# One core, a hybrid decoder trunk: values and probabilities turned through DRAM in another key order, and the first norm's gains carried in x's own rows

## The chip, the cores and the metric

The kernel runs on one core of a Trainium2 chip. A core has TensorE (matrix products, called PE in the profile, with its weight loads as PEld), VectorE (DVE), ScalarE (ACT), GpSimd (POOL) and SyncE (SP), which share an on-chip memory of 128 partitions and 16 DMA engines. DMAs are issued from the queues of SP, ACT and POOL. The metric is the time of one execution on the device, in microseconds; less is better.

## What is computed

A trunk of two layers on 272 tokens (16 learned meta tokens and 256 of the input), width 2048, 16 heads of 128. Layer 0 is forgetting attention and a squared-ReLU MLP; layer 1 is stick-breaking attention with its own shared keys and values, and another MLP. The final norm is given out for the 256 tokens.

```python
def rms_norm(x, g):
    y = x * lax.rsqrt(jnp.mean(x * x, axis=-1, keepdims=True) + RMS_EPS)
    return y * g
...
h = concatenate([meta_tokens, x])                       # 272 x 2048
for layer in range(2):
    a = rms_norm(h, norm_attn[layer])
    if layer == 0:                                      # forgetting attention
        q, k, v, f_logit = split(a @ fox_w_in[0])
        cum_logf = cumsum(log_sigmoid(f_logit + fox_b_f[0]))
        p = softmax(q k / sqrt(128) + cum_logf[query] - cum_logf[key], keys up to the query)
        h = h + (p v) @ fox_w_o[0]
    else:                                               # stick-breaking attention
        k, v = split(rms_norm(h, kv_norm) @ w_kv)
        z = (a @ sb_w_q[0]) k / sqrt(128)
        p = exp(log_sigmoid(z) + sum of log_sigmoid(-z) over later keys before the query)
        h = h + (p v) @ sb_w_o[0]
    h = h + square(relu(rms_norm(h, norm_mlp[layer]) @ w_up[layer])) @ w_down[layer]
return rms_norm(h, final_norm)[16:]
```

In both attentions p v is a sum over keys. It comes out the same in any order of the keys, as long as p and v have the same one.

## The kernel before, in words

**Activations** stand with features on the partitions: `hT` is the residual stream, 16 chunks of 128 features by 272 tokens in float32. A norm is split in two: the gain is multiplied onto a chunk when it is split for the products (`split_chunk`), and the factor per token is multiplied onto the results.

**Products.** Every float32 operand is split into a rounded part (hi) and the rest (lo), and three products hi·hi, hi·lo, lo·hi replace one. Weights come as blocks of 128 x 512 by DMA on SP's queue (`raw`), ScalarE makes `whi` (L210), VectorE `wlo` (L211). A `gemm_group` is 512 output features: four quarters `kb` of the input features, 48 products each, 192 in all, with all tokens as the moving columns: 272 in layer 0 and for layer 1's keys and values, 256 (without the meta tokens, `t0 = M`) elsewhere in layer 1. A few products are issued six columns wider, on zeros beside the row (`wide`). Groups are numbered by `u` in program order: 1 to 12 are layer 0's q, k, v, 13 to 16 its output projection, 17 to 48 its MLP, 49 to 52 layer 1's queries, 53 to 60 its keys and values, 61 to 64 its output projection, 65 on its MLP. The last group is computed with tokens on the partitions (`token_group`).

**Order.** The framework's planner orders the instructions of each engine by simulated times. The code ties it down: products of a group (but for the first) keep their order, and other instructions are put behind the product with a given number of the group (`behind(ins, issued[140])`).

**The start.** Nine idle products on a constant (each two passes in the trace) run on TensorE before the data is there (L61). In the first group `load_x` (L314) issues x's chunks on SP's queue in turn with the weights, and the gains of all six norms (`g_sb`, L318) right after x's first chunk; the first block of weights goes on ACT's queue (L197). `load_gates` (L336) loads the forget gates' bias and weights on ACT's queue in the second quarter and multiplies the gate weights by the first norm's gains; their products come after the first group.

**Heads.** Heads are worked in four groups of four, each as two pairs. Values come out of the products with features on the partitions, while p v needs keys there. VectorE turns 32 x 32 squares (`squares`, `turn_probabilities`), and a trip through DRAM moves the squares: `scratch` writes the values of a pair (`turned` to `v_dram`) with four DMAs, one for every 32 partitions, in pieces of 512 bytes; `values_read` reads them back as 128 rows of 2 KB; `values_back` splits them. Probabilities go the same way, `turn_probabilities` (four DMAs a pair) and `probabilities_back`, with pieces of 768 bytes and rows of 3 KB. In layer 0 both use POOL's queue, in layer 1 the probabilities use SP's. The weighted sums of a group (`po`) are computed during a later group. The last four heads of a layer have no later attention group: `last_heads` puts their reads, splits and products between the products of the first group of the output projection, at given numbers (`reads`, `uses`, `places`). That projection needs the results (`x_o`) of the first pair from product 144 on and of the second pair from 168 on. In layer 1 the second pair of the last heads is written from ACT's queue. `to_token_major` uses `scratch` too, for the last 512 features of the residual stream.

Of the kernel before, what the change touches and what calls it, by code (L numbers as in the profile page):

```python
# [15 lines left out]
P = 128  # L16
# [17 lines left out]
def yoco_kernel(ctx: ExitStack, tc: tile.TileContext, hT_in, gains, b_f, w_f, w_qkv0, w_o0, w_up, w_dn,  # L34
# [16 lines left out]

    hT = const.tile([P, NC, T], F32, name="hT")
    g_sb = const.tile([P, 6, NC], F32, name="g_sb")
# [5 lines left out]
    idle = patt.tile([P, 512], F32, tag="patt", name="idle")  # L59
    for _ in range(9):  # L60
        nc.tensor.matmul(idle[:, :P], mean_w, mean_w, start=True, stop=True)  # L61
# [60 lines left out]
    def split_chunk(sp, gi, c):  # L122

        g = g_sb[:, gi, c:c + 1]
        nc.scalar.activation(sp.hi[:, c], hT[:, c, sp.t0:], AF.Copy, scale=g)
        nc.vector.scalar_tensor_tensor(out=sp.lo[:, c], in0=hT[:, c, sp.t0:], scalar=g,
                                       in1=sp.hi[:, c].bitcast(F32), op0=ALU.mult, op1=ALU.subtract)
# [87 lines left out]
    def gemm_group(wblk, sp, t0, evac, before={}, after={}, load_x=None, between={}):  # L215
# [7 lines left out]
        for kb in range(4):  # L223
# [16 lines left out]
            for kcs, ms in runs:  # L240
# [6 lines left out]

                wide = [(0, 0, 0), (1, 0, 1), (2, 1, 1)] if t0 and u % 4 == 1 else []
                if u == 61:
# [64 lines left out]
    def load_x(chunks):  # L314
        c0, n = chunks[0], len(chunks)
        nc.sync.dma_start(hT[:, c0:c0 + n, :], hT_in[:, c0:c0 + n, :])
        if c0 == 0:
            nc.sync.dma_start(g_sb, gains)  # L318
        for c in chunks:
            split_chunk(xa, G_A0, c)  # L320
# [15 lines left out]
    def load_gates(wf_sb, wf, both):  # L336
        nc.scalar.dma_start(bf_sb, b_f)
        nc.scalar.dma_start(wf_sb, w_f)
        nc.vector.tensor_tensor(out=wf[:, :, :NC], in0=wf_sb, in1=g_sb[:, G_A0, :].unsqueeze(2).to_broadcast([P, NC, NC]), op=ALU.mult)

# [51 lines left out]
    def scratch(t, products, queues=(nc.gpsimd, nc.gpsimd)):  # L392
        for pr in range(2):
            y = t[:, pr].rearrange("p (c x) -> p c x", c=4)
            for a in range(4):
                ins = queues[pr].dma_start(v_dram[pr].rearrange("c j a x -> a j c x")[a], y[32 * a:32 * a + 32])
                behind(ins, products[pr])

    def values_read(t, pr, read, queue=nc.gpsimd):
        ins = queue.dma_start(t[:, pr], v_dram[pr].rearrange("c j a x -> (c j) (a x)"))  # L400
        behind(ins, read)
        return ins.ins
# [66 lines left out]
    def turn_probabilities(s, raw, pr, queue):  # L469

        y = raw[:, :768].rearrange("p (c h b i) -> p c h b i", c=4, h=2, b=3)
        for i in range(2):
            for b, o in enumerate((0, 144, 144 + P)):
                nc.vector.transpose(y[:, :, i, b, :], s[:, 2 * pr + i, o:o + P].rearrange("p (c k) -> p c k", c=4))
        y = y.rearrange("p c h b i -> p c (h b i)")
        for a in range(4):
            queue.dma_start(p_dram[pr].rearrange("c j a x -> a j c x")[a], y[32 * a:32 * a + 32])

    def probabilities_back(pps, places, queue):
        for pr, at in enumerate(places):  # L480
            raw, p0 = pps[pr]
            behind(queue.dma_start(raw[:, :768], p_dram[pr].rearrange("c j a x -> (c j) (a x)")), issued[at])

# [258 lines left out]
    for g in range(4):  # L742
# [43 lines left out]
        turned = squares(vT, "pp", f"1_{g}")  # L786
        if g < 3:
            scratch(turned, issued[-2:])
        else:
            scratch(turned, (issued[-20], issued[-1]), (nc.gpsimd, nc.scalar))  # L790

# [47 lines left out]

    box["last"] = last_heads(turned, (36, 60), (84, 116), (120, 146), "1_3", nc.gpsimd, pair1, corner1)  # L840

# [11 lines left out]
    def to_token_major():  # L853
        t = squares(hT[:, 12:, M:], "pp", "h")
        scratch(t, issued[-2:])
        return t
# [131 lines left out]
```

## Time and profile before

| | |
|---|---|
| median of 3 runs | 2265.85 us (2265.61 to 2266.42) |
| the profiled execution | 2264.61 us, its span 2262.9 us |
| TensorE's products, share of the span | 2255.1 us, 100% |
| VectorE | 1355.1 us, 60% |
| ScalarE | 1056.6 us, 47% |
| GpSimd | 120.5 us, 5% |
| DMA | 435.94 MB, mean 193 GB/s |

The span is from the first to the last instruction; the execution's time has some 1.7 us around it. Every time in the profile counts from the span's start. Matmuls overlap, so one product's duration in the trace (some 280 ns) is longer than its share of the time; the pace is read from counts of products in a stretch. A row of the timeline is start, duration, engine, line, operation, out<-in, shape and count, and in brackets the idle time of the engine before it with what ended it. A row of the chain of waits is start, duration and what the end of the kernel waited for there. A row of waits is who waited for whom, with the total, the times and the longest. A q behind an engine's name is its queue.

### The profile page before, as it was taken

Reading aid. Unit: us, or ns where it says so; the run is one execution under the profiler, and the core shown is the slowest. Engines: PE = TensorE matmul, PEld = TensorE weight load, DVE = VectorE, ACT = ScalarE, POOL = GpSimd, SP = SyncE. Lnnn points to the kernel's source line nnn. Section 1 sums busy time; section 2 is a strip of 40 time slices with the busy share of each in tenths; the row PEclk is TensorE's granted clock in tenths of the full one; section 3 lists DMA queues with packets and bytes.
Section 4 is the critical chain, followed back from the end, with each engine's and each line's share of the span. In section 5 each row is a group of like instructions: output and inputs, shape, how many; then the busy total and the mean of one; then the engine's idle time right before and its main releaser. Section 6 shows DMA issues by size and latency. Waiting matters only on the chain.

```text
span 2262.9 us, 45001 instructions
## 1 busy us (share of the span) xinstructions
PE 2255.1 (100%) x18785; PEld 2247.0 (99%) x18785; DVE 1355.1 (60%) x1989; ACT 1056.6 (47%) x1440; POOL 120.5 (5%) x236
## 2 busy tenths in 40 slices
PE   9999999999999999999999999999999999999998
PEld 9999999999999999999999999999999999999998
DVE  7777676554455455455566688766555555555555
ACT  6444445453354344344444455555544543543554
POOL 1321210000000000000000011200000000001001
PEclk9999999999999999999999999999999999999999
DMA  7766765555555555555555566665656656566664
GB/s 242 238 201 192 227 208 170 186 169 184 179 177 180 175 176 185 173 184 178 170 192 183 180 220 219 213 218 188 198 186 197 198 192 197 186 197 209 197 199 141
DMA packets 131852, 435.94 MB, mean 193 GB/s; under 512 B 18528, under 2 KB 26352, under 8 KB 131648
## 3 DMA queue, kind: packets, MB, share of 16 engines
q1 hardware_dynamic: 122112, 413.57, 56.1%
q0 software_dynamic: 6640, 15.80, 2.3%
q10 hardware_dynamic: 2896, 3.69, 0.5%
q8 instruction: 147, 2.41, 0.4%
q14 instruction: 57, 0.47, 0.1%
HBM read 419.22 MB, written 13.78 MB: 191 GB/s over the span
## 4 chain that ended last, share of the span: by engine, by line
PE 98%; DMA 1%; DVE 0%; issue 0%; ACT 0%; POOL 0%; SPq 0%; POOLq 0%; ACTq 0%
PE acc L177 96%; PE po L415 0%; PE pz L415 0%; PE ps L415 0%; DMA raw<-w_o 0%; DMA turned<-v_dram 0%; DMA raw<-w_qkv 0%; PE pz L764 0%; PE ps L541 0%; DVE wlo L211 0%; PE po L618 0%; PE po L812 0%; ACT whi L210 0%; PE pf L346 0%; POOL ob L887 0%
## 5 line engine op out<-in xcount | busy, mean ns | idle before, releaser
L211 DVE TENSOR_TENSOR wlo<-raw,whi 128x1024 fp32r<-128x1024 f32 (+1 forms) x774 | 928.4, 1215 | 693.1 <-ACT whi L210 685.9
L210 ACT ACTIVATE whi<-raw 128x1024 fp32r<-128x1024 f32 (+1 forms) x774 | 796.7, 1049 | 984.6 <-PE acc L177 947.3
L177 PE MATMUL acc<-x_m,whi 128*128 128x272 f32 (+1 forms) x4096 | 642.9, 281 | 0.0
L177 PE MATMUL acc<-x_u,whi 128*128 128x272 f32 (+1 forms) x3968 | 626.0, 281 | 0.0
L177 PEld LDWEIGHTS acc<-x_m,whi 128*128 128x128 f32 x4096 | 565.7, 188 | 0.1
L177 PEld LDWEIGHTS acc<-x_u,whi 128*128 128x128 f32 x3968 | 550.1, 188 | 0.0
L177 PE MATMUL acc<-x_m,wlo 128*128 128x272 f32 (+1 forms) x2048 | 440.7, 281 | 0.0
L177 PE MATMUL acc<-x_u,wlo 128*128 128x272 f32 (+1 forms) x1984 | 431.5, 281 | 0.0
L177 PE MATMUL acc<-x_a,whi 128*128 128x272 f32 (+1 forms) x2048 | 352.3, 285 | 0.2 <-ACT whi L210 0.2
L177 PEld LDWEIGHTS acc<-x_m,wlo 128*128 128x128 f32 x2048 | 323.2, 188 | 0.0
L177 PEld LDWEIGHTS acc<-x_u,wlo 128*128 128x128 f32 x1984 | 315.1, 188 | 0.0
L177 PEld LDWEIGHTS acc<-x_a,whi 128*128 128x128 f32 x2048 | 300.2, 188 | 1.5 <-issue 0.9
L177 PE MATMUL acc<-x_a,wlo 128*128 128x272 f32 (+1 forms) x1024 | 252.9, 285 | 0.0
L177 PE MATMUL acc<-x_kv,whi 128*128 128x272 f32 x1024 | 193.2, 288 | 0.0
L177 PEld LDWEIGHTS acc<-x_a,wlo 128*128 128x128 f32 x1024 | 175.4, 188 | 0.6 <-issue 0.4
L177 PE MATMUL acc<-x_o,whi 128*128 128x272 f32 (+1 forms) x1024 | 162.4, 282 | 0.5 <-ACT x_o L466 0.3
L177 PEld LDWEIGHTS acc<-x_kv,whi 128*128 128x128 f32 x1024 | 160.7, 188 | 0.0
L177 PE MATMUL acc<-x_kv,wlo 128*128 128x272 f32 x512 | 146.9, 287 | 0.0
L177 PEld LDWEIGHTS acc<-x_o,whi 128*128 128x128 f32 x1024 | 142.1, 188 | 0.8 <-ACT x_o L466 0.5
L295 DVE TENSOR_TENSOR hT<-acc,hT 128x272 f32<-128x272 f32 (+1 forms) x156 | 67.3, 432 | 73.2 <-PE acc L177 73.0
L177 PE MATMUL acc<-x_o,wlo 128*128 128x272 f32 (+1 forms) x512 | 110.4, 281 | 0.0
L177 PEld LDWEIGHTS acc<-x_kv,wlo 128*128 128x128 f32 x512 | 96.4, 188 | 0.0
(221 smaller groups left out, 1120.9 us busy)
## 6 DMA issues: line engine op xcount, KB each, us to landing
raw<-w_up SPq DMA_DIRECT2D x256, 512.0 KB, 4.0
raw<-w_dn SPq DMA_DIRECT2D x256, 512.0 KB, 4.3
raw<-w_qkv SPq DMA_DIRECT2D x92, 512.0 KB, 4.4
raw<-w_o SPq DMA_DIRECT2D x64, 512.0 KB, 4.4
raw<-w_kv SPq DMA_DIRECT2D x64, 512.0 KB, 4.3
raw<-w_q SPq DMA_DIRECT2D x32, 512.0 KB, 4.3
v_dram<-turned POOLq DMA_DIRECT2D x56, 64.0 KB, 3.9
turned<-v_dram POOLq DMA_DIRECT2D x14, 256.0 KB, 5.3
```

Source lines behind the costliest of these rows:

```text
L177: ins = nc.tensor.matmul(*args, **kw).ins
L210: on_act = nc.scalar.activation(hp, src, AF.Copy)
L211: on_dve = nc.vector.tensor_tensor(out=lp, in0=src, in1=hp.bitcast(F32), op=ALU.subtract)
L295: nc.vector.tensor_tensor(out=hT[:, c, t0:], in0=acc, in1=hT[:, c, t0:], op=ALU.add)
```

## The change

- **Key order.** `scratch` and `turn_probabilities` write a pair with one DMA, each partition's 2 or 3 KB in one piece. The reads gather four pieces of 512 or 768 bytes per partition, so key 32c + j of a block of 128 stands on partition 4j + c instead of 32c + j. Probabilities and values get the same order. `to_token_major`, whose order is that of the tokens, keeps the old four writes.
- **Queue and places.** The second pair of layer 1's last heads is written from POOL's queue, as the first. Its last heads' `uses` go from (84, 116) to (70, 106), their `places` from (120, 146) to (112, 132).
- **Wide products.** Group 62 gets the three wide products that every fourth group has, and the two groups that finish a norm in their third quarter with 256 columns (49 and 65) get two more each.
- **Gains in x's rows.** A row of `hT` is four columns longer; column 272 holds the first norm's gain, which the host appends to x as a 273rd token. `load_x` loads 273 columns. The first norm's splits take the gain from there. `g_sb` is loaded in `load_gates`, on ACT's queue.
- **Idle products.** Seven instead of nine.

```diff
-    hT = const.tile([P, NC, T], F32, name="hT")
+    hTg = const.tile([P, NC, T + 4], F32, name="hTg")
+    hT = hTg[:, :, :T]
...
-    for _ in range(9):
+    for _ in range(7):
         nc.tensor.matmul(idle[:, :P], mean_w, mean_w, start=True, stop=True)
...
     def split_chunk(sp, gi, c):
-        g = g_sb[:, gi, c:c + 1]
+        g = g_sb[:, gi, c:c + 1] if gi != G_A0 else hTg[:, c, T:T + 1]
...
-                wide = [(0, 0, 0), (1, 0, 1), (2, 1, 1)] if t0 and u % 4 == 1 else []
+                wide = [(0, 0, 0), (1, 0, 1), (2, 1, 1)] if t0 and (u % 4 == 1 or u == 62) else []
+                if t0 and 2 in before:
+                    wide = wide + [(2, 0, 0), (2, 1, 0)]
...
     def load_x(chunks):
-        nc.sync.dma_start(hT[:, c0:c0 + n, :], hT_in[:, c0:c0 + n, :])
-        if c0 == 0:
-            nc.sync.dma_start(g_sb, gains)
+        nc.sync.dma_start(hTg[:, c0:c0 + n, :T + 1], hT_in[:, c0:c0 + n, :])
...
     def load_gates(wf_sb, wf, both):
         nc.scalar.dma_start(bf_sb, b_f)
         nc.scalar.dma_start(wf_sb, w_f)
+        nc.scalar.dma_start(g_sb, gains)
...
     def scratch(t, products, queues=(nc.gpsimd, nc.gpsimd)):
         for pr in range(2):
-            y = t[:, pr].rearrange("p (c x) -> p c x", c=4)
-            for a in range(4):
-                ins = queues[pr].dma_start(v_dram[pr].rearrange("c j a x -> a j c x")[a], y[32 * a:32 * a + 32])
-                behind(ins, products[pr])
+            ins = queues[pr].dma_start(v_dram[pr].rearrange("a j c x -> (a j) (c x)"), t[:, pr])
+            behind(ins, products[pr])

     def values_read(t, pr, read, queue=nc.gpsimd):
-        ins = queue.dma_start(t[:, pr], v_dram[pr].rearrange("c j a x -> (c j) (a x)"))
+        ins = queue.dma_start(t[:, pr].rearrange("p (a x) -> p a x", a=4), v_dram[pr].rearrange("a j c x -> (j c) a x"))
...
     def turn_probabilities(s, raw, pr, queue):
-        y = y.rearrange("p c h b i -> p c (h b i)")
-        for a in range(4):
-            queue.dma_start(p_dram[pr].rearrange("c j a x -> a j c x")[a], y[32 * a:32 * a + 32])
+        queue.dma_start(p_dram[pr].rearrange("a j c x -> (a j) (c x)"), raw[:, :768])

     def probabilities_back(pps, places, queue):
-            behind(queue.dma_start(raw[:, :768], p_dram[pr].rearrange("c j a x -> (c j) (a x)")), issued[at])
+            behind(queue.dma_start(raw[:, :768].rearrange("p (a x) -> p a x", a=4), p_dram[pr].rearrange("a j c x -> (j c) a x")), issued[at])
...
-        if g < 3:
-            scratch(turned, issued[-2:])
-        else:
-            scratch(turned, (issued[-20], issued[-1]), (nc.gpsimd, nc.scalar))
+        scratch(turned, issued[-2:] if g < 3 else (issued[-20], issued[-1]))
...
-    box["last"] = last_heads(turned, (36, 60), (84, 116), (120, 146), "1_3", nc.gpsimd, pair1, corner1)
+    box["last"] = last_heads(turned, (36, 60), (70, 106), (112, 132), "1_3", nc.gpsimd, pair1, corner1)
...
     def to_token_major():
-        scratch(t, issued[-2:])
+        for pr in range(2):
+            y = t[:, pr].rearrange("p (c x) -> p c x", c=4)
+            for a in range(4):
+                behind(nc.gpsimd.dma_start(v_dram[pr].rearrange("c j a x -> a j c x")[a], y[32 * a:32 * a + 32]), issued[-2 + pr])
...
-        "hT_in": _feature_major(np.concatenate([meta_tokens, x[0]], axis=0)),
+        "hT_in": _feature_major(np.concatenate([meta_tokens, x[0], norm_attn[:1]], axis=0)),
```

## The prediction

> **What bounds the kernel now.** I read the page's first part, then TensorE's own waits, then stretches of the span with their product counts, and last the chain of waits.
>
> ```profile
> span 2262.9 us, 45001 instructions
> PE 2255.1 (100%) x18785; PEld 2247.0 (99%) x18785; DVE 1355.1 (60%) x1989; ACT 1056.6 (47%) x1440; POOL 120.5 (5%) x236
> ```
> ```profile
> PE acc L177 <- ACT x_o L466: 0.3, 1, 0.3
> PE acc L177 <- ACT whi L210: 0.2, 1, 0.2
> PE acc L177 <- DVE x_o L467: 0.2, 1, 0.2
> ```
> ```profile
> 7.13:30.00 22.87, 22.87 (x195) 21.18 (x196) 22.16 (x41) 19.89 (x41) 0.00 (x0) 1.00 0.92 324
> 424.00:1180.00 756.00, 756.00 (x6139) 756.00 (x6138) 396.74 (x484) 326.26 (x419) 0.27 (x1) 1.00 0.55 178
> 1467.00:1486.00 19.00, 18.54 (x156) 17.82 (x156) 11.83 (x17) 8.92 (x15) 3.19 (x7) 1.00 0.86 280
> 1486.00:1566.00 80.00, 80.00 (x707) 80.00 (x707) 53.25 (x77) 42.55 (x63) 0.27 (x1) 1.00 0.57 185
> ```
>
> TensorE is busy all but 7.8 us of 2262.9 and of its waits for another engine only the three shown lie between its first real product and the tail. In the stretch table the second number is TensorE's busy time with its count of products, the last two are the DMA engines' share and GB/s. A 272-column product takes 756.00 / 6139 = 123.1 ns, a 256-column one 80.00 / 707 = 113.2 ns. No part of the change removes a real product, so it can gain only where TensorE is short of work. There are two such places ahead of the tail. One is the start, before 7.13 us. The other is the stretch 1467 to 1486, the last heads of layer 1: 156 products at 113.2 ns are 17.66 us, so about 1.3 us of the 19.00 are lost. All other gains land on engines with spare time.
>
> **The start.** The chain of waits begins on SP's queue, and TensorE's rows beside it show what it did meanwhile:
>
> ```profile
> 0.81 0.38 SPq L316
> 1.24 0.42 SPq L318
> 1.71 0.43 SPq L316
> 2.18 4.46 DMA raw<-w_qkv
> 6.67 0.42 ACT whi L210
> 7.13 16.74 PE acc L177 x132
> ```
> ```profile
> 1.12 4.21 PE L61 MATMUL idle<-mean_w 128*128 128x128 f32 x18 [1.12 <-DVE mean_w L57]
> 4.98 1.07 PE L177 MATMUL acc<-x_a,whi 128*128 128x272 f32 x5
> 5.89 0.29 PE L177 MATMUL acc<-x_a,wlo 128*128 128x272 f32 x1
> ...
> 6.50 0.41 PE L177 MATMUL acc<-x_a,wlo 128*128 128x272 f32 x2
> ```
> ```profile
> 3.90 0.42 ACT L210 ACTIVATE whi<-raw 128x256 fp32r<-128x256 f32 x1 [1.81 <-DMA raw<-w_qkv]
> 4.22 0.51 ACT L125 ACTIVATE x_a<-hT,g_sb 128x272 fp32r<-128x272 f32 x1
> ```
>
> The gains' load (L318) stands between x's first two rows on SP's queue. Without it the second row and the weights behind it are issued 1.71 - 1.24 = 0.47 us sooner. They land sooner by 0.47 at most, and by nothing if the DMA engines rather than the issue set the landing. TensorE has the first chunk's twelve products done at about 6.75 and starts the next at 7.13, so it can use 0.38 of this, and a little more if the first chunk itself starts earlier.
>
> The two idle products are four of the 18 passes (each float32 product is two). 4.21 us over 18, less the last one's tail, is 0.213 us a pass, so TensorE is free 0.85 us earlier, at about 4.3. The first x row is split at 4.22 + 0.51 = 4.73, so the first real product can start near 4.8 instead of 4.98: at most 0.2 us. That x's split no longer waits for the gains gains nothing more: it starts at 4.22, behind the weights' split on ScalarE, and that one waits for its own load until 3.90.
>
> Further on the start is a matter of DMA: from 7.13 to 30 us the DMA engines are 0.92 busy at 324 GB/s.
>
> ```profile
> 16.28 1.06 ACT L210 ACTIVATE whi<-raw 128x1024 fp32r<-128x1024 f32 x1 [0.32 <-DMA raw<-w_qkv]
> ```
>
> This split, the first of the group's third quarter, waits 0.32 us for its load and ends at 17.34; by the order of products TensorE comes to it at about 17.6. So of a gain at 7.13 only some 0.26 us passes this place. The load's bytes ahead of it hardly change: 48 KB of gains leave (0.15 us at 324 GB/s), x grows by one column in 272, or 8 KB, and four of its loads fall from one 2,176-byte piece per partition into two of 1,092. The gains come back on ScalarE's queue as a third small load behind the gate weights; its 0.35 us of issue runs beside ScalarE's own work, as the two before it do, and its only early reader is the scaling of the gate weights on VectorE at 22.0. If it lands later than that, VectorE's x splits queue behind it. Bounds of the start: -0.5 and, for loads that got slower, +0.4. I take -0.2, nearest to the 0.26 that the row at 16.28 lets through.
>
> The first passes run at half the pace of later ones: 0.213 us against 2.62 / 22 = 0.12 for the same product in the tail:
>
> ```profile
> 2253.57 2.62 PE L177 MATMUL idle_fin<-mean_w 128*128 128x128 f32 x22
> ```
>
> The pace changes near 5.4: five products take from 4.98 to 5.89, 0.18 us each, those after them 0.12. The change puts a hole of 0.5 us (4.3 to 4.8) into the work ahead of this. The Trainium skill, "TensorE: Matmul & The Clock Gate", Part 1, says that the clock is halved by default and is released after a window of about 3.4 us of sustained activity, whose start is free-running. It speaks against taking idle products away; the trace agrees with the half pace, and no run here shows what a hole does. By it the estimate is one window more at half pace, 1.7 us, and the sum would be +1.7 - 0.9 (the last heads' term below) = +0.8.
>
> **The last heads of layer 1.** Here is the chain through that stretch, and the engines' rows for the second pair of heads:
>
> ```profile
> 1476.76 5.22 DMA turned<-v_dram
> ...
> 1485.10 0.61 DVE x_o L467
> 1485.75 81.02 PE acc L177 x712
> ```
> ```profile
> 1465.43 2.20 POOL L396 DMA_DIRECT2D v_dram<-turned  x4 [0.50 <-DVE turned L389]
> ...
> 1471.21 0.56 POOL L400 DMA_DIRECT2D turned<-v_dram  x1 [1.92 <-DMA v_dram<-turned]
> 1476.76 0.55 POOL L400 DMA_DIRECT2D turned<-v_dram  x1 [4.99 <-DVE wlo L211]
> ```
> ```profile
> 1467.31 2.83 ACTq L396 DMA_DIRECT2D v_dram<-turned  x4
> ...
> 1482.00 0.42 ACT L377 ACTIVATE v<-turned 128x256 fp32r<-128x256 f32 x1 [2.48 <-DMA turned<-v_dram]
> ```
> ```profile
> 1482.47 0.84 PE L415 MATMUL po<-p,v 128*128 128x256 f32 x3
> ```
>
> The page's DMA issues (KB of each, median us to landing):
>
> ```profile
> v_dram<-turned POOLq DMA_DIRECT2D x56, 64.0 KB, 3.9
> turned<-v_dram POOLq DMA_DIRECT2D x14, 256.0 KB, 5.3
> p_dram<-raw_p POOLq DMA_DIRECT2D x32, 96.0 KB, 3.5
> ```
>
> The second pair's values are written by four DMAs from ScalarE's queue (to 1470.14), read back at 1476.76, there at 1482.0; its products start at 1482.47, and the output projection then waits for their split (x_o) twice. The change writes them with one DMA from POOL's queue, issued when the transposes are done, near 1467.3. With the median landing of a write, 3.9 us, the read can go at about 1471.5 and lands near 1477 to 1478, four us earlier. The products are moved forward from place 146 to 132, 14 x 0.113 = 1.6 us, and the consumers of x_o stay where they are: both waits go. The first pair is moved up by 8 places, 0.9 us. Its write is one issue, not four (three of 0.55 us less), so its read can start about 1 us sooner and just keeps up. Behind each of these reads stand ScalarE's weight splits: if values asked for at places 70 and 106 are late, ScalarE's queue stops; it has the time, since in the row at 1482.00 it stood idle for 2.48 us. Bounds: -1.3 (all that is lost) and +0.7 (the first pair a full move late). I take -0.9: the second pair's loss goes, and something of the first pair's is late next.
>
> **The key order elsewhere.**
>
> Four writes with 512- or 768-byte pieces become one with 2- or 3-KB pieces; the reads turn from 2 or 3 KB a piece to four of 512 or 768 bytes. POOL issues 15 value writes instead of 56 and 8 of probabilities instead of 32; at 0.55 us each that is 36 us of POOL, which is 5% busy: nothing on the path. SP drops 24 + 3 issues, which only lets weights go out sooner. One write of 256 KB should land after 3.9 to 5.3 us, the medians of 64 KB and of the large read above; three issues fewer give back 1.65. The reads get longer by an amount that no row shows: between nothing and, if they went like four writes in a row, 1.65 us. The Trainium skill, "DMA: Bandwidth & Descriptors", Rules for kernel authors, says to join many small transfers into a large one; its fixed 2 us and 436 GB/s would make the joined write an estimated 0.45 us longer than a small one. The trace's medians say up to 1.4; the sum stays the same. What covers it is the distance to the products:
>
> ```profile
> 1319.34 0.57 POOL L400 DMA_DIRECT2D turned<-v_dram  x1 [4.94 <-DMA v_dram<-turned]
> ...
> 1323.59 0.42 ACT L377 ACTIVATE v<-turned 128x256 fp32r<-128x256 f32 x1 [0.62 <-DMA turned<-v_dram]
> ...
> 1327.07 0.28 PE L415 MATMUL po<-p,v 128*128 128x256 f32 x1
> ```
>
> This is the tightest full group, in layer 1: values there at 1323.6, used at 1327.07, with 1.5 us of splitting between. 2 us are to spare, and the write lands sooner. I cost it at 0.
>
> **Small parts.** Seven more products of 262 columns (three in the second group of the last projection, two each in two groups with a norm): some 3 ns each, 0.02 us.
>
> ```profile
> L177 PE MATMUL acc<-x_m,wlo x992: 276/276/279, 1568.9 to 2165.5; 128*128 128x256 f32 x197, 128*128 128x262 f32 x2
> ```
>
> hT's rows are 1,104 bytes apart instead of 1,088, and everything allocated after it moves by 16 x 16 = 256 bytes. I take 0.
>
> **Sum:** -0.2 - 0.9 + 0.02 = -1.1 us. The profiled execution took 2264.61 (span 2262.9 and 1.7 around it), which gives 2263.5; the median of the runs shown, 2265.85, is 1.24 above it, so 2264.8.
>
> **The rivals.**
> - *The clock comes up later.* The hole counts as idleness, and half pace lasts on. One stretch like the first (1.12 to 5.4) more would cost 4.3 / 2 = 2.1 us: -1.1 + 0.2 + 2.1, about 2267.1. For it: the half pace. Against it: the hole is 0.5 of 4.3 us.
> - *The first pair is late.* The moved places ask for values that are not there, TensorE waits up to 0.7 us and the gain of 0.9 becomes a loss: about 2266.4.
> - *The reads in small pieces are slow* (slower than before). In each of six full groups and two last ones the second pair's products wait. It decides from 2 us longer than now, the spare time above; at 3 us longer it costs 8 x 1 us, about 2273. Against it: the write is issued and lands sooner by more than a us.
> - *The move by 256 bytes changes the pace of products.* A 256-column product at the 262-column one's pace (+3.3 ns) over layer 1's 47 groups of 192 would be +30 us, one period of four groups 2.5. It can go the other way as well: layer 0's 123.1 ns is 9.9 above the 256-column product's for 16 columns more, and 3 ns less over some 12,000 products is -36. Against it: the two buffers of x's rows are 41,216 bytes apart, 256 more than a multiple of 512, and x_m and x_u in them run alike.
>
> **How the numbers follow.** Main course 0.55, the first pair late 0.12, the clock 0.10: these are within 0.2% (4.5 us, about what a measurement of this kernel can tell from no change), together 0.77. Slow reads 0.10 and a worse pace 0.08 are slower: 0.18. A better pace 0.05 is faster. The main course alone reaches from 2263.4 (both bounds' gains and 0.6 of scatter) to 2266. The range has to take in the late pair and the clock, to 2267.1 with 1 us for their bounds: 2263.2 to 2268.2; it leaves out the pace and the larger part of slow reads, 0.2.
>
> **What would show it.** Right: SP's second issue at 1.24; first real product near 4.8 and the next chunk near 6.7; then nothing left of most of it at 17.6; in the last heads no wait for x_o, the second pair's read landed by 1478, and the stretch 1467 to 1486 holding some eight products more. Wrong: passes of 0.21 us or products of 0.18 after 5.9; waits of TensorE for values in the groups; or a product time other than 123.1 and 113.2 ns.

## The result and the profile after

The changed kernel is slower by 1.3%: 2294.51 us (median of five executions; 2289.99 to 2299.13) against 2265.85 us (median of five; 2265.61 to 2266.42), a ratio of 1.0126 with a 95% interval of 1.0109 to 1.0143. The forecast of 2264.8 us, within 0.2% of before, was wrong. The profiled execution took 2289.99 us, the fastest of its runs, so its profile explains 25.4 us of the 28.7.

The first lines of the page after:

```profile
span 2288.3 us, 44814 instructions
PE 2263.8 (99%) x18781; PEld 2253.2 (98%) x18781; DVE 1352.3 (59%) x1989; ACT 1056.4 (46%) x1440; POOL 90.9 (4%) x171
```

POOL is busy for 30 us less than before, as forecast, and TensorE for 8.7 us more, with the same real products. So TensorE both stood idle longer and ran slower for a while. Its waits name the first (engine, tile and line, waited for, us in total, times, longest):

```profile
PE pom L598 <- DMA vm_sb<-m_dram: 14.7, 3, 6.5
PE acc L178 <- DVE vT L503: 1.6, 3, 0.6
```

Neither is in the list of before. `pom` is the small product of layer 0's groups for the first 16 tokens and the corners; `vm_sb` holds the rows it needs, which GpSimd writes to DRAM (`m_dram`, L460) and reads back (L462). Stretches of the changed kernel around the second of these waits, cut at 3.41 us (stretch: its length, TensorE busy and products, granted clock, DMA share, GB/s):

```profile
190.89:194.30 3.41, 0.80 (x7) 1.00 0.33 132
194.30:197.71 3.41, 1.56 (x7) 0.50 0.61 190
197.71:201.12 3.41, 3.41 (x18) 0.50 0.52 161
201.13:204.54 3.41, 3.41 (x30) 1.00 0.00 0
```

TensorE stands from 191.69 to 196.15, and the clock is at 0.50 from 194.30 to 201.13. The same five products of p and v, which take 0.57 us before (184.59 to 185.16), take 1.07 here (197.02 to 198.09). So part of the wait is paid again behind it. The clock's record shows such half stretches behind all three waits, of 3.41, 6.83 and 6.83 us, and between the start and the last two microseconds nowhere else. With TensorE busy for 3.2, 5.0 and 4.1 us of them, half of that is lost: 6.1 us.

Everywhere else the pace of products is that of before; here a stretch of 272-column products before, and the one of the changed kernel 25 us later:

```profile
430.00:1180.00 750.00, 750.00 (x6091) 1.00 0.55 178
```
```profile
455.00:1205.00 750.00, 750.00 (x6090) 1.00 0.54 178
```

In layer 1's last stretch of 256-column products both kernels do 5734 in 650 us (before from 1560.00, after from 1585.25). The two programs can be compared stage by stage, by the starts of the same products in both profiles: the start (to the first group's scores), layer 0's attention (to its output projection), layer 1's attention in two parts, and the rest. In us:

| stage | before | after | |
|---|---|---|---|
| start | 57.5 | 58.4 | +0.9 |
| layer 0's attention | 256.1 | 279.6 | +23.4 |
| layer 1's four groups, to the output projection | 182.9 | 184.1 | +1.2 |
| output projection with the last heads | 91.3 | 90.6 | -0.7 |
| all the rest | 1675.1 | 1675.6 | +0.5 |

Layer 0's 23.4 us are 14.7 of waits for `vm_sb`, 6.1 at half clock, 1.6 of waits for `vT`, and about 1 us that I can't assign.

Why `vm_sb` is late stands in GpSimd's rows. In the second group before, and after (start, us, engine, line, out<-in, times, and in brackets the idle time before it and what ended it; "issue" means that the profile shows nothing that was waited for):

```profile
165.99 0.56 POOL L400 DMA_DIRECT2D turned<-v_dram  x1 [0.18 <-issue]
166.59 0.60 POOL L460 DMA_DIRECT2D m_dram<-vt  x1
...
171.30 0.57 POOL L400 DMA_DIRECT2D turned<-v_dram  x1
176.54 0.71 POOL L462 DMA_DIRECT2D vm_sb<-m_dram  x1 [4.67 <-DMA m_dram<-vt]
```
```profile
172.65 0.57 POOL L396 DMA_DIRECT2D v_dram<-turned  x1 [0.19 <-issue]
173.26 0.76 POOL L400 DMA_DIRECT2D turned<-v_dram  x1
180.70 0.77 POOL L400 DMA_DIRECT2D turned<-v_dram  x1 [6.68 <-issue]
181.47 0.60 POOL L460 DMA_DIRECT2D m_dram<-vt  x1
185.80 1.75 POOL L460 DMA_DIRECT2D m_dram<-vt  x3 [3.73 <-issue]
193.66 0.71 POOL L462 DMA_DIRECT2D vm_sb<-m_dram  x1 [6.11 <-DMA m_dram<-vt]
```

The reads of values at L400 are the ones that the change cut into 512 pieces (128 before). GpSimd stood 6.7 us ahead of the second one and 3.7 us among the row writes behind it, for nothing that the profile names. And the planner's order on this queue is another: before, the row writes stood between the two reads, now behind both. The read of the rows goes out 17.1 us later than before, in a kernel that is 7.5 us behind when TensorE gets there; of the 9.6 us between them 4.4 were to spare (in before issued at 176.54, some 3.3 us of transfer by the page's median, used at 184.22), and the read itself was 0.8 shorter (used 2.5 us after its issue). That leaves the wait of 4.46.

### The profile page after: what moved, and what is told of

It is laid out like the page before. It is cut to its first block, busy times and chain, and to the rows that moved or that the text cites. A ratio compares the mean times of both kernels' runs of the same rounds, so it can differ in the third digit from the quotient of the medians.

```text
span 2288.3 us, 44814 instructions
## 1 busy us (share of the span) xinstructions
PE 2263.8 (99%) x18781; PEld 2253.2 (98%) x18781; DVE 1352.3 (59%) x1989; ACT 1056.4 (46%) x1440; POOL 90.9 (4%) x171
## 5 line engine op out<-in xcount | busy, mean ns | idle before, releaser
L298 DVE TENSOR_TENSOR hTg<-acc,hTg 128x272 f32<-128x272 f32 (+1 forms) x156 | 67.1, 431 | 73.3 <-PE acc L178 73.1
```

The source lines that it names most:

```text
L298: nc.vector.tensor_tensor(out=hT[:, c, t0:], in0=acc, in1=hT[:, c, t0:], op=ALU.add)
```

## The experiments

Two theories stood against each other, with a third behind them. *Room*: GpSimd can only issue a DMA when the descriptors of its pieces (the records of what to move) find room, which the program sets (`dynamic_dma_scratch_size`, 1024), and two reads of 512 pieces don't fit. *Order*: the small urgent transfers now stand behind large ones on one in-order queue, and that is enough. *Slow reads*: the rival of the prediction, that small pieces simply take longer.

**The room alone, on the changed kernel and on the kernel before (runs 1 and 4).** The 1,088 bytes that more room needs come from letting the norm's `y` lie in its result; in the changed kernel the order of work on every engine stays the same.

```
-            y = tmp.tile([P, T], F32, tag="rs_y", bufs=1, ...)
+            y = r[:, self.t0:]
...
-    nc = bacc.Bacc("TRN2", ..., dynamic_dma_scratch_size=1024)
+    nc = bacc.Bacc("TRN2", ..., dynamic_dma_scratch_size=2048)
```

> The changed kernel with twice the room for the descriptors of the software queue (scratch 2048 instead of 1024 bytes a partition; the 1,088 bytes that this needs come from letting the norm's intermediate y lie in the tile of its result). The order on every engine stays that of the changed kernel. Theory (the queue's room: GpSimd cannot issue the second values read of 512 pieces until the first has landed, and the four writes of the meta tokens' and corners' rows and their read stand behind it): the second read is issued within 1 us of the first (6.7 us later in the changed kernel), TensorE waits for vm_sb 0 us (14.7 us now), no half-clock stretch after 7 us (17.1 us now), time 2264 to 2268 us. Rival (the reads in small pieces are slow as transfers, or the queue carries them one after the other): the wait for vm_sb stays within 2 us of 14.7 and the time stays at 2288 to 2296 us.

> The kernel before with the same larger room for descriptors and the same move of y, as the control of the first run. Theory: TensorE waits for nothing in these groups with the small room either, so nothing changes: 2265 to 2267 us. Rival (the larger room or the move of y speeds the kernel up by itself): 2263 us or less.

Run 1: 2273.98 us, ratio to before 1.0035 (1.0022 to 1.0048); run 4: 2266.52 us, 0.9999 (0.9989 to 1.0008). So the room is worth 20.5 us in the changed kernel and nothing in the one before. It is also what GpSimd stood for without a name: its idle time put down to "issue" falls from 42.9 us to none ahead of the value reads and from 12.2 to 0.4 ahead of the row writes, and in the kernel before, where the row writes stood for 7.6 us in all, to none in run 4. *Slow reads* falls as the main cause: with the same pieces most of the loss is gone. But *room* alone misses its number by 6 us. In run 1 the second read waits for its own write only, and still 5.7 us of waits for `vm_sb` and 2.4 for `vT` are left. The second have to do with VectorE's multiplication of the corners (`pm_sb`); here are VectorE's rows of run 1, and those of the kernel before:

```profile
PE pom L598 <- DMA vm_sb<-m_dram: 5.7, 3, 2.9
PE acc L178 <- DVE vT L503: 2.4, 2, 1.3
```
```profile
164.94 0.29 DVE L449 TENSOR_TENSOR pm_sb<-pmq,maskD 128x128 f32<-128x128 f32 x1 [5.93 <-DMA pmq<-c_dram]
...
166.29 0.43 DVE L503 TENSOR_TENSOR vT<-acc,rstd_a 128x272 f32<-128x272 f32 x1
```
```profile
160.74 0.44 DVE L505 TENSOR_TENSOR vT<-acc,rstd_a 128x272 f32<-128x272 f32 x1 [0.50 <-PE acc L177]
...
162.41 0.38 DVE L449 TENSOR_TENSOR pm_sb<-pmq,maskD 128x128 f32<-128x128 f32 x1
```

In run 1 VectorE stands 5.9 us for the corners' read (`pmq`), and the four evacuations of `vT` (its copies of the values out of TensorE's results), which TensorE needs, stand behind it. In the kernel before the multiplication comes behind the fourth evacuation, and VectorE doesn't wait for it in layer 0. The read itself is not late: in the changed kernel it is issued as soon as its own write has landed, and it lands 3.1 us sooner than before if both are counted from the same product (165.82 in a kernel 6.5 us behind there, against 162.39). What is new is the planner's order on VectorE, in groups 2 to 4 of the changed kernel and of run 1.

**The order (runs 2, 5 and 6).** Run 2 puts the rows' writes ahead of both reads in the changed kernel, run 5 adds the larger room to that, and run 6 leaves room and order as they are but moves layer 0's small transfers (`c_dram`, `pmq`, `m_dram`, `vm_sb`) to SP's queue.

```
-            rows_turned([vm, vc], vm_sb, issued[112], issued[130], f"0_{g}")
+            rows_turned([vm, vc], vm_sb, issued[88], issued[130], f"0_{g}")
```

> The changed kernel with the four writes of the meta tokens' and corners' rows placed 24 products earlier in layer 0, so that GpSimd issues them ahead of both values reads; the read of these rows stays behind the second values read. Theory (the queue's room): the rows' writes no longer wait, but the first values read waits for room behind them and the second still waits for the first, so the rows' read is issued only some 0.8 us after the second values read, 3 to 6 us earlier than now; about half the wait for vm_sb goes and the values of the second pair may come late instead: 2270 to 2285 us. Rival (only the order is wrong, the room is enough): all of the wait goes, 2265 to 2267 us. Rival (slow reads): 2288 to 2296 us.

> The changed kernel with both the larger room for descriptors and the rows' four writes ahead of the values reads. The larger room alone took 15.0 us off the median (2289.0 to 2274.0 by the medians of profiled and timed runs of one kind) and left 5.7 us of waits for vm_sb; the early rows alone left 0.5 us of them but 3.5 us of waits for the second values. Theory (two things add up: the room, and that the small transfers stand behind the large ones on one in-order queue): with both, TensorE waits under 1 us for vm_sb and under 1 us for v in layer 0; what remains is the start (+1.2 us) and the wait for vT's evacuation (2 to 4 us, since VectorE still stands for the corners' read pmq on the same queue): 2267 to 2271 us. Rival (the reads of 512 pieces are slow however they are queued): the waits for v stay at 3 us or more, 2272 us or more.

> The changed kernel with layer 0's small transfers (corner write and read c_dram and pmq, rows' writes m_dram and read vm_sb) on SP's hardware queue; probabilities and values stay on GpSimd's software queue with the small room. Theory (the loss is small transfers held up behind large ones): no wait of TensorE for vm_sb (14.7 us in the changed kernel), VectorE waits under 2 us in all for pmq (10.5 us), and the second values read still stands 6 to 7 us for the first, so a wait for v of 1 to 2 us a group may come in its place: 2267 to 2273 us. Rival (the values reads themselves are the cause): 2280 us or more. Counter-effect to watch: SP stands at these transfers' semaphores and weights go out later (a wait of whi for raw).

Run 2: 2276.58 us, 1.0043 (1.0028 to 1.0058); run 5: 2271.74 us, 1.0026 (1.0016 to 1.0036), 0.7 us over its range; run 6: 2273.77 us, 1.0029 (1.0017 to 1.0041), 0.8 over. (The 15.0 us that the expectation of run 5 speaks of should read 20.5.) In run 2, with the small room, 0.5 us of waits for `vm_sb` are left, not the half that was expected: in layer 0 the order alone takes this wait away, as the rival had it. Its 3.5 us of waits for the second values don't come in its place. They are all in layer 1, which run 2 leaves as the changed kernel has it. What keeps its time up is layer 1 (5.7 us more than before), `vT` (3.6) and the start (1.2). So what held `vm_sb` up is both things at once: rows behind the reads, and reads that stand for room. In run 5 the waits for `vm_sb` and for values are under a microsecond (the two last rows here are in layer 1), and what is left of TensorE's waits in layer 0 is the `vT` that stands behind `pmq`:

```profile
PE acc L178 <- DVE vT L503: 3.5, 3, 1.4
...
PE po L415 <- ACT v L379: 0.4, 1, 0.4
PE po L415 <- DVE v L380: 0.3, 1, 0.3
```

Run 6 is the cleanest: with the small room and the reads as slow as ever, layer 0's attention takes 256.3 us, against 256.1 before and 279.6 in the changed kernel. So all of layer 0's loss came through these four small transfers. The rows of `vm_sb` were held up behind large reads, and the room sets for how long. For `pmq` this was not the reason: I had expected VectorE's wait for it to fall below 2 us without the large reads ahead of it, and it was 12.4. But it landed 1.4 us sooner than in run 1, counted from the same product of the second group, and TensorE did not wait for what stood behind it. What run 6 keeps is lost elsewhere: 2.7 us at the start and 6.6 in layer 1.

**How the room counts (runs 10 and 12).** Run 10 gives the changed kernel 1152 instead of 1024, run 12 gives the kernel before 512. Nothing else differs, but for the `y` of run 1 in run 10.

> The changed kernel with room for 1152 instead of 1024 bytes of descriptors. Theory in numbers: a piece takes 16 bytes of a ring, the pieces of one DMA are spread over 16 rings with one more each, so a read of 512 pieces takes 33 places of a ring and there are 64 places now, 72 here: two reads (66) do fit, and the second is issued as soon as its own write has landed and not at the first one's landing (6.7 us after the first now); the rows' writes (17 places each) don't fit beside them and wait for the first read to land, so the wait for vm_sb stays, a little shorter: 10 to 15 us, time 2284 to 2294 us. Rival (not pieces count, one large transfer is taken at a time, or the room comes in coarser steps): the second read still stands 6 to 7 us.

> The kernel before with half the room, 512 bytes or 32 places by the count above, and nothing else changed. Theory: the rows' four writes (17 places each) now go one at a time, the last some 10 us later, and the kernel before gets the wait of the changed one: 5 to 10 us for vm_sb in each of three groups, and half-clock stretches behind them, 2280 us or more. Rival (room matters only with the new pieces): 2265 to 2267 us.

Run 10: 2287.84 us, 1.0093 (1.0074 to 1.0111); run 12: 2314.03 us, 1.0208 (1.0190 to 1.0227). GpSimd's rows of run 10 in the second group:

```profile
173.94 0.76 POOL L400 DMA_DIRECT2D turned<-v_dram  x1
178.00 0.77 POOL L400 DMA_DIRECT2D turned<-v_dram  x1 [3.30 <-DMA v_dram<-turned]
180.19 1.18 POOL L460 DMA_DIRECT2D m_dram<-vt  x2 [1.42 <-DVE wlo L212]
186.31 1.16 POOL L460 DMA_DIRECT2D m_dram<-vt  x2 [4.94 <-issue]
```

With an eighth more room the second read goes 4.1 us after the first, as soon as its own write has landed, and two row writes instead of one fit in before GpSimd stands again. So the limit lies between 1024 and 1152 for two such reads, and it goes by pieces: a read of the same bytes in 128 pieces never stood for more than 0.2 us in the kernel before. The count used in the expectation comes from the Trainium skill, "DMA: Bandwidth & Descriptors": 16 bytes a descriptor (Terms), and one more per engine for the completion (The descriptor swizzle). By it a read of 512 pieces, spread over 16 engines, needs an estimated 33 places and two of them 66; there are 64 at 1024 and 72 at 1152. The rows of runs 10 and 12 agree with it; they don't prove the single numbers.

Run 12 shows the same without any change in key order: in the kernel before with half the room, the row writes go one at a time,

```profile
194.45 0.61 POOL L460 DMA_DIRECT2D m_dram<-vt  x1 [3.16 <-issue]
198.67 0.58 POOL L460 DMA_DIRECT2D m_dram<-vt  x1 [3.61 <-issue]
```
```profile
209.91 0.69 PE L600 MATMUL pom<-s0T,vm_sb 128*128 128x64 f32 x2 [8.37 <-DMA vm_sb<-m_dram]
```

and TensorE waits for `vm_sb` 25.7 us in three groups, where with 1024 it waits for nothing.

**Layer by layer (runs 3, 7 and 11).** Run 3 is the changed kernel with layer 0's key order of before; run 7 has only layer 1 changed (its key order, places, queue and wide products); run 11 is run 7 with the larger room.

```
+            if old:
+                y = t[:, pr].rearrange("p (c x) -> p c x", c=4)
+                for a in range(4):
+                    behind(queues[pr].dma_start(v_dram[pr].rearrange("c j a x -> a j c x")[a], ...), products[pr])
+                continue
```

> The changed kernel with layer 0's values and probabilities in the key order of the kernel before (four small writes, one read of 128 pieces); the start, layer 1 and the places stay changed. Theory: the 14.7 us of waits for vm_sb and the half-clock stretches behind them go, what is left is the start (+0.9 us), layer 1's full groups (+0.5 to +0.8 us) and the gain of the last heads (-0.7 us): 2266 to 2268 us. Rival (the loss comes from the rows of x made 4 bytes longer or from the shifted addresses, wherever they are used): 2280 us or more.

> The kernel before with the change in layer 1 alone: its key order, the places of its last heads, the single queue for their writes and the wide products; the start and layer 0 are those of before. By my prediction: -0.9 us, 2265 us. Theory now: the two values reads of 512 pieces don't fit together in the queue's room here either; in the full groups the corners' read stands behind them. From the stage times of the changed kernel: full groups +0.8 us together, last heads -0.3 us, and in some executions a wait and with it a half-clock stretch of 3.4 us: 2266 to 2270 us, with more spread than the kernel before.

> The seventh run's kernel (the change in layer 1 alone, 2271.2 us) with the larger room. Theory (layer 1's loss is the room too): the full groups take 52.4 to 53.1 us again (53.3, 53.3 and 53.7 in the seventh run), no waits for v, time 2264.5 to 2266.5 us. Rival (small pieces are slow reads): 2269 us or more.

Run 3: 2271.99 us, 1.0026 (1.0016 to 1.0036), 4 us over its range; run 7: 2271.18 us, 1.0021 (1.0011 to 1.0030), 1 us over; run 11: 2265.89 us, 0.9999 (0.9990 to 1.0009). Layer 0 is back at 256.2 us in run 3. Both misses have one cause: I had read layer 1's loss off one profile of the changed kernel, where it was small. It varies from execution to execution; in the profiles of runs 2, 3, 6 and 7 it is made of waits of 0.4 to 2.0 us for values, and of the half clock behind the longest of them:

| layer 1, to the end of its output projection, us | profiles |
|---|---|
| order of before (before, runs 4, 8, 14) | 273.9 to 275.4, mean 274.5 |
| changed, small room (after, runs 2, 3, 6, 7) | 274.6, 279.8, 279.0, 280.7, 278.2 |
| changed, larger room (runs 1, 5, 9, 11, 13) | 272.7 to 274.2, mean 273.6 |

With the larger room the four groups take 182.73 us in each of the five profiles; with the small one 184.1 to 189.3.

**The start (runs 8, 9, 13 and 14).** In the changed kernel the gains come as a third load on ScalarE's queue, behind the two for the gates. ScalarE's rows there, and in run 8, which has the changed start on the kernel before but loads the gains from GpSimd's queue (`nc.gpsimd.dma_start(g_sb, gains)`):

```profile
13.65 0.35 ACTq L339 DMA_DIRECT2D wf_sb<-w_f  x1
14.97 0.33 ACTq L340 DMA_DIRECT2D g_sb<-gains  x1
15.35 0.75 ACT L143 ACTIVATE sq_a<-hTg 128x272 f32<-128x272 f32 x2 [1.77 <-DMA raw<-w_qkv]
```
```profile
13.68 0.62 ACT L211 ACTIVATE whi<-raw 128x512 fp32r<-128x512 f32 x1
14.21 0.74 ACT L143 ACTIVATE sq_a<-hTg 128x272 f32<-128x272 f32 x2
```

In the program this third load waits for a semaphore that one of the weights' loads uses as well, and it is issued when that load lands. Behind it stood the split of the weights that TensorE came to at 17.6. Run 9 puts all the remedies into the changed kernel: the larger room, the rows first, the gains on GpSimd's queue, and the multiplication that waits for `pmq` placed behind the evacuations. Runs 13 and 14 are runs 9 and 8 with nine idle products again.

```
+            behind(pm_ins, issued[20])
...
-        nc.scalar.dma_start(g_sb, gains)
+        nc.gpsimd.dma_start(g_sb, gains)
```

> The kernel before with the changed start alone (gain column in x's rows, seven idle products), but the table of gains loaded from GpSimd's queue and not as the third load on ScalarE's. In the four profiles with the changed start, ScalarE stands 1.7 to 1.9 us at that third load, for a semaphore that a weights load still holds, and the scores of the first group begin at 58.45 to 59.23 us (57.51 and 57.77 with the start of before). Theory (the loss of the start is that wait): ScalarE's hole near 13.5 to 15.3 us is gone, TensorE does not wait for whi at 17 to 18 us, and the first scores begin at 57.0 to 57.6 us; time 2265 to 2266 us. Rival (the longer rows of x, or the clock): 58.3 us or later.

> The changed kernel with every cause found so far taken away: the larger room and the rows' writes ahead of the values reads (as in the fifth run), VectorE's multiplication that waits for the corners' read pmq placed behind the evacuations of vT (it stands 18.1 us in front of them in the fifth run), and the gains loaded from GpSimd's queue (as in the eighth). Theory: no wait of TensorE for vT (3.5 us in the fifth run) or vm_sb, first scores at 57.0 to 57.9 us, layer 1's full groups 52.4 to 52.6 us each, the last heads -0.3 us; the change then does what it was forecast to do: 2264 to 2266 us. Rival (the reads in small pieces also cost by themselves, hidden so far by the other waits): waits for v come up in layer 0 or 1 and the time is 2268 us or more.

> The mended kernel of the ninth run with nine idle products again. Theory (with seven, TensorE stands 0.2 to 0.7 us between the last idle product and the first real one, and where this hole is 0.3 us or more the clock comes up 3.4 us later): no hole, clock full by 7 us, first scores at 57.2 to 57.9 us (59.17 in the ninth run), time 2262.5 to 2265 us, about 0.1% below the kernel before. Rival (the clock's rise is chance and the idle products don't matter): full speed at 8 us or later can come here too, time 2265 us.

> The kernel of the eighth run (the kernel before, with the gain column in x's rows and the table of gains on GpSimd's queue) with nine idle products again. Theory: no hole, clock full by 7 us, first scores at 57.0 to 57.6 us (57.49 in the eighth run, whose hole was 0.27 us and whose clock was full at 6.16), time 2263.5 to 2266 us, less spread than the eighth run's 3.9 us. Rival as for the thirteenth run.

| | median, us | ratio to before (95%) | clock full at | first scores at |
|---|---|---|---|---|
| run 8: start, gains from GpSimd, 7 idle | 2264.61 | 0.9993 (0.9984 to 1.0003) | 6.16 | 57.49 |
| run 14: the same, 9 idle | 2265.93 | 0.9999 (0.9990 to 1.0008) | 7.34 | 57.75 |
| run 9: all remedies, 7 idle | 2265.03 | 0.9994 (0.9986 to 1.0003) | 10.34 | 59.17 |
| run 13: all remedies, 9 idle | 2264.52 | 0.9994 (0.9985 to 1.0003) | 5.48 | 58.49 |

(The clock is full from the first such entry in its record on.) ScalarE's hole is gone in run 8 and the first scores are back where they were before (57.51; 57.51 to 58.16 in the five profiles with the start of before). In runs 9 and 13 they are not, against what was expected: run 9's clock came up late, and run 13, with an early clock, still waits 0.6 us for `whi`, for the most part because ScalarE stands 1.09 us for a load of x ahead of that split, and is at 58.49. Layer 0's attention takes 256.2 us in runs 9 and 13, that of before. So with these causes taken away the change is what the forecast said it would be: no difference that can be measured. None of these kernels is shown to beat the one before.

The idle products show in TensorE's rows. Here the start of run 8 and of run 9, which issue the same work:

```profile
1.12 3.36 PE L62 MATMUL idle<-mean_w 128*128 128x128 f32 x14 [1.12 <-DVE mean_w L58]
4.75 1.27 PE L178 MATMUL acc<-x_a,whi 128*128 128x272 f32 x4 [0.27 <-ACT whi L211]
...
6.39 0.76 PE L178 MATMUL acc<-x_a,whi 128*128 128x272 f32 x4
```
```profile
4.78 1.27 PE L178 MATMUL acc<-x_a,whi 128*128 128x272 f32 x4 [0.30 <-ACT whi L211]
...
6.52 1.27 PE L178 MATMUL acc<-x_a,whi 128*128 128x272 f32 x4
```

In run 9 the products stay at half pace, four in 1.27 us, when those of run 8 are already at 0.76. Of nine profiles with seven idle products the clock came up at 4.99 to 6.57 us in five, in which TensorE stood 0.19 to 0.27 us ahead of the first real product, and at 8.65 to 10.34 in four, in which it stood 0.30 to 0.71. In seven profiles with nine it stood there once, for 0.15 us, and the clock was up at 4.19 to 7.34 in all of them. So a late clock goes with a hole from about 0.3 us on, and run 13 against run 9 fits: no hole, and an early clock. The holes ended when ScalarE had split the first weights. The expectations of runs 13 and 14 hold for their totals; the first scores came 0.6 and 0.15 us later and run 14's clock 0.3 later than forecast.

## Why the prediction was wrong, step by step

- **The start, -0.2 us forecast: +0.9 measured** (58.45 against 57.51; 0.3 to 0.9 against the five profiles with the start of before). SP's second issue came at 1.25 and the first real product at 4.66, as forecast, and TensorE ran ahead until 17.6. What failed is the sentence that the third load's "0.35 us of issue runs beside ScalarE's own work, as the two before it do". Its duration was right; that it had to wait was not looked for. I followed its data to the reader at 22.0 us and not what is queued behind it on its own engine. Without that wait the change gains nothing at the start either (57.49 and 57.75 in runs 8 and 14, against 57.51).
- **The clock up later, a rival at 2267.1 with a chance of 0.10.** True in four profiles of nine, so likelier than I put it, and cheaper: run 9's first scores came 1.7 us after run 8's but 0.7 after run 13's, and where ScalarE's hole covers it only some 0.5 us of it shows (58.8 to 59.2 in runs 1, 5 and 10, against 58.4 to 58.7 in the changed kernel and runs 2 and 3).
- **The last heads of layer 1, -0.9 us forecast: -0.7 in the profile of the changed kernel, but +1.2 in the full groups ahead of them.** No wait for `x_o` is left and the stretch holds six more products instead of eight. But the second pair's read was there one microsecond sooner, not four: GpSimd had the corners' copies to do before it issued the write, and the read itself stood for room.

```profile
1493.45 1.60 POOL L433 COPY pk_vc<-vT 128x64 f32<-128x64 f32 x2
1495.01 0.55 POOL L396 DMA_DIRECT2D v_dram<-turned  x1
1495.55 0.75 POOL L400 DMA_DIRECT2D turned<-v_dram  x1
1501.40 0.77 POOL L400 DMA_DIRECT2D turned<-v_dram  x1 [5.10 <-issue]
```

  With the products at place 132 moved 1.6 us forward, that left little to spare: they waited 2.0, 1.9 and 1.4 us for these values in runs 3, 6 and 7 and 0.1 in the changed kernel (0.6 and 1.0 in runs 13 and 9, with the larger room). The rival had named the first pair (2266.4, chance 0.12); that pair hardly waited, the second was the late one. With room enough, layer 1 as a whole gains 0.9 us on the mean of five profiles against four (two thirds of it in the stretch of the last heads, 90.8 against 91.4), but the single values overlap. So the waits for `x_o` went as forecast, the path of the read was misjudged by 3 us, and the size of the gain is not shown.
- **The key order elsewhere, 0 forecast: +23.4 us in layer 0 and 0 to 6 in layer 1.** This is the step that failed. Three sentences of it did: "SP and POOL" were priced by the time of their issues, and for that POOL indeed got freer; "What covers it is the distance to the products" was measured for the values alone, in layer 1; and "I cost it at 0" named no work queued behind the reads. In layer 0 the rows of `vm_sb` stand behind them on the same queue. They had 4.4 us to spare, and in the second group their read came 9.6 us later, counted from the product that needs it. That the planner may order the queues and VectorE anew was not priced either; the smaller waits, for `vT`, came from that. The joined write was no part of the loss: it landed after a median of 3.3 us, sooner than the 3.9 to 5.3 forecast.
- **The slow reads, a rival at 2273 with a chance of 0.10.** In the changed kernel a read in 512 pieces landed after a median of 5.6 us; one in 128 pieces took 5.3 in the kernel before (the prediction shows that row):

```profile
turned<-v_dram POOLq DMA_DIRECT2D x14, 256.0 KB, 5.6
```

  With the larger room, where two reads are in flight together, the median is 6.2 to 7.1 us in runs 1, 5, 9 and 13, against 5.3 to 5.9 in the four with the order of before (before, runs 4, 8 and 14). So small pieces may cost about 1 us a read, less than the 2 us that were to spare, and in run 9 the kernel is no slower for it. The rival had the right sign and the wrong place: in layer 0 what waits is not the values' products but what is issued behind the reads. In layer 1 the values' products do wait, and with more room they don't (run 11).
- **The pace of products, chances 0.08 and 0.05: refuted**, 6091 and 6090 products in 750 us, and 5734 in 650 us in both at 256 columns. The 256 bytes and the wide products cost nothing that shows.
- **The price of a wait.** I priced each late microsecond at one. In layer 0 the 14.7 us of waiting cost 6.1 more at half clock, and this differs from execution to execution, which goes with the spread of 9 us in the changed kernel against 1 in the one before in the same comparison.

## What to carry to other kernels

Cutting a transfer into more pieces can take room on GpSimd's queue, not only time: follow there what is issued behind it, and price the most urgent small transfer by its own spare time, not the transfer that was changed. An added DMA issue can cost its engine the wait for its semaphore as well as its issue; look at what stands behind it on that engine. The planner's order of the small instructions on GpSimd and VectorE changed with it, though the edit didn't ask for that: compare each engine's order before and after. And a wait of TensorE of some 2 us can cost nearly twice its length, since the clock can halve behind it.

## What was unexpected in the hardware

**When the clock halves.** The clock changes on a fixed grid of 3.41 us within an execution, and what decides is how much of a slot TensorE stood idle. Run 1 has both cases, in slots of its own grid: idle for 1.62 us of one slot and 1.30 of the next (one wait of 2.92 us) it kept full speed; idle for 2.01 us within one slot, a shorter wait, it ran at half for the next.

```profile
107.74:111.15 3.41, 1.79 (x15) 1.00 0.74 263
111.15:114.56 3.41, 2.11 (x18) 1.00 0.10 22
189.66:193.07 3.41, 1.40 (x12) 1.00 0.43 171
193.07:196.48 3.41, 3.41 (x18) 0.50 0.43 129
```

Run 6 narrows it: 1.65 us idle kept full speed, 1.89 did not.

```profile
1326.31:1329.72 3.41, 1.76 (x15) 1.00 0.15 52
...
1486.75:1490.16 3.41, 1.52 (x13) 1.00 0.80 294
1490.17:1493.57 3.40, 3.40 (x16) 0.50 0.33 89
```

In all sixteen profiles, no slot at full speed with 1.67 us of idle time or less is followed by half speed, and each of those with 1.89 or more is. So a wait of 1.9 us can cost 1.7 us more, and one of 2.9 nothing more, by where it falls on the grid. The Trainium skill, "TensorE: Matmul & The Clock Gate", Why this matters for your kernels, asks for no idle gaps above about 3 us; here a gap of 1.9 us was enough, and the measurement decides. The way up asks for a fuller slot. At the start a slot with 0.31 us idle or more kept the clock at half for another one in four profiles (runs 1, 5, 9 and 10), and one with 0.27 or less did not. Run 12 shows that this bound is not sharp: its first full slot had 0.34 us idle, ahead of the first product. Later in run 12 a slot with 0.29 us idle went back to full speed, and one with 0.91 did not.

**GpSimd's room for descriptors** can cost a kernel much in which GpSimd is 4% busy: 20.5 us went with 1024 more bytes of it, and 47.5 us came to the kernel before with 512 fewer.
